# Asking for the background transfers on GpSimd's queue instead of the sync queue

## The chip, the core and the metric

The kernel runs on one core of a Trainium2 chip. A core has five engines that run side by side, each working through its own list of instructions in order: TensorE (PE, matrix products; its weight loads are PEld), VectorE (DVE), ScalarE (ACT), GpSimd (POOL) and SyncE (SP), which here does nothing but ask for transfers. An instruction waits at the head of its engine's list until the semaphores it needs are set, and everything behind it on that engine waits with it. That is true of a transfer's request as well: it stands in the list of the engine that issues it. The metric is device time of one execution in microseconds (us), lower is better.

## The reference: what is computed

One layer of a diffusion backbone over 2048 latent tokens of width 1024, with a context of 256 tokens ahead of them, all in float32:

```python
ada = silu(c) @ w_ada + b_ada            # 6 vectors of 1024: sh1, sc1, g1, sh2, sc2, g2
h   = modulate(rmsnorm(x, norm_mix), sh1, sc1)
o   = token_mixers(h @ w_in, ...)        # gated recurrence (4 heads) and gMLP gating (4 heads)
x   = x + g1 * (o @ w_out)
h2  = modulate(rmsnorm(x, norm_ffn), sh2, sc2)
x   = x + g2 * conv_ffn(h2, w_up, conv_w, conv_b, w_down)
out = rmsnorm(x, norm_final)
```

Of `ada`, the first two vectors are needed at once; `g1`, `sh2`, `sc2`, `g2` only after the token mixers. The kernel folds the gates into weights: `w_out * g1` and `w_down * g2` are formed once, in the background of the token mixers, and parked in DRAM.

## The kernel before, in words

The products are done in three float32r passes (high times high, high times low, low times high), so each weight tile is split into a high part (`S.copy` to `whi`, L125, on ACT) and a low part (`wlo`, L126, on DVE or POOL).

The first 960 us or so are the token mixers. TensorE projects `h` with 128 columns of `w_in` at a time: a bank is eight steps of three matmuls (`pj`). For each new group of columns a raw tile of 512 KB is loaded (L207, on SP), split, and used. Between the steps of a bank two pumps may each put in a piece of other work. One pump carries the heads: the recurrence's score products (`sc`), transposes (`mi`), norms and gates. The other, `bg_q`, carries the background, one generator after another:

- `ada_block(e)`, e = 0 to 7: 512 columns of `w_ada` for `g1`, `sh2`, `sc2`, `g2`. Four raw tiles of 512 KB (L877) are multiplied into a row sum on DVE (L885); the bias row comes first (L871), and four of the eight blocks store their result into the small DRAM tensor `g_d` (L895).
- `w_down_ops`: 22 pieces of `w_down` (L939), each multiplied by `g2` (L941, DVE) and stored to `wd_d` (L942); `g2` is read back twice from `g_d` (L936).
- `w_out_ops`: 16 pieces of `w_out` (L915) with the matching `g1` (L916), multiplied (L925, DVE), split (ACT, then DVE) and stored to `wo_d` in two halves (L927, L928).

A generator's `yield 7.0` means that its next piece is put in once about 7 us of matmuls have been written behind it. The background's raw tiles and the raw tiles of `w_in` are the same three buffers (`raw_tile`, tag `raw`, bufs=3), taken in turn. So a load of `w_in` may have to wait until a background piece has been stored out of the buffer that it gets.

The order on each engine is made by a scheduler when the program is built. It plays the program through with costs of its own and writes each engine's instructions down in the order in which they came up; `pin` fixes the relative order of some. On the chip this order is fixed, whatever the real times are.

POOL's own work in this part is small: the two steps of each reciprocal root (L118 a multiply-add, L120 a power), wanted by the norms of the recurrence's output (`on`, L698) and of the gating (`nt`, L671 and L673); the gating's last product (L647); and the zeroing of the row sums (L870). After the token mixers the background is done, and the rest of the kernel has none of the changed lines in it.

Of the kernel before, what the change touches and what calls it, by code (L numbers as in the profile page):

```python
# [18 lines left out]
P = 128  # L19
# [31 lines left out]
def view(t, off, dims):  # L51

    return bass.AP(t.tensor, t.offset + off, [list(t.ap[0])] + [list(d) for d in dims])
# [24 lines left out]
def tile_trunk(ctx, tc, x, c, cx, c_ctx, w_ada, b_ada, norm_mix, norm_ffn, w_in, hg_norm, sgu_g, sgu_b,  # L78
               w_sp, b_sp, w_out, w_up, conv_w, conv_b, w_down, norm_final, masks, out):
    nc = tc.nc  # L80
    V, S, G, T = nc.vector, nc.scalar, nc.gpsimd, Tensor(nc.tensor)
    ld = nc.sync.dma_start
    st = nc.sync.dma_start
    pin = tc.keep_in_program_order

    x = x[0]
    w_ada, w_in, w_out, w_up, w_down = w_ada[0], w_in[0], w_out[0], w_up[0], w_down[0]
# [19 lines left out]
    g_d = dr.tile([2, D], F32, name="g_d")  # L107
# [3 lines left out]
    wo_d = dr.tile([P, NK, 2, D], F32, name="wo_d")  # L111
    wd_d = [dr.tile([P, 2, D], F32, name=f"wd{j}") for j in range(NF // 2)]
# [10 lines left out]
    def split(hi, lo, raw, eng=None, keep=lambda i: i):  # L123

        keep(S.copy(hi, raw))  # L125
        (eng or G).tensor_sub(lo, raw, hi.bitcast(F32))  # L126
# [56 lines left out]
    with es1:  # L183
# [13 lines left out]
        def bank(tag):  # L197
            return ps.tile([P, 512], F32, tag=tag, name=tag, bufs={"pj": 3, "sc": 2, "mi": 3}[tag])

        def raw_tile():  # L200
            return p1.tile([P, D], F32, tag="raw", name="raw", bufs=3)
# [54 lines left out]
        acc = ph.tile([P, 2, 512], F32, tag="S", name="acc")  # L256
# [609 lines left out]
        def ada_block(e):  # L866

            col = 2 * D + e * 512
            acc = pm.tile([P, 512], F32, tag="acc", name="acc")
            G.memset(acc, 0.0)  # L870
            ld(acc[0:1, :], b_ada[0:1, col:col + 512])  # L871
            wts = []

            def load(k):
                if k < 8:
                    wt = raw_tile().rearrange("p (k c) -> p k c", k=2)
                    ld(wt, w_ada[:, col:col + 512].rearrange("(p k) e -> p k e", k=8)[:, k:k + 2, :])  # L877
                    wts.append(wt)
            load(0)
            yield 4.0  # L880
            for k in range(0, 8, 2):
                load(k + 2)
                wt = wts.pop(0)
                for i in range(2):
                    pin(V.scalar_tensor_tensor(out=acc, in0=wt[:, i, :], scalar=cs2[:, k + i, 0:1], in1=acc,  # L885
                                               op0=ALU.mult, op1=ALU.add))
                yield 3.2
            yield 3.0
            pa = bank("mi")
            hf_ = e % 2  # L890
            if e in (0, 1, 6, 7):
                T.matmul(pa[:1, :], ones[:, :1], acc, start=True, stop=True)
                gr = pm.tile([P, 512], F32, tag="ot", name="gr", bufs=2)
                S.copy(gr[:1, :], pa[:1, :])
                st(g_d[e // 6:e // 6 + 1, hf_ * 512:hf_ * 512 + 512], gr[:1, :])  # L895
            else:
                for j in range(4):
                    T.matmul(pa[:, 2 * j:2 * j + 2], acc[:, j * P:(j + 1) * P], ones[:, :2], start=True, stop=True)
                if e in (2, 3):
                    V.tensor_copy(s2[:, hf_ * 4:hf_ * 4 + 4], pa[:, 0:8:2])  # L900
                else:
                    V.scalar_tensor_tensor(out=a2[:, hf_ * 4:hf_ * 4 + 4], in0=pa[:, 0:8:2], scalar=1.0,
                                           in1=nffn[:, hf_ * 4:hf_ * 4 + 4], op0=ALU.add, op1=ALU.mult)
            yield 0.0

        def w_out_ops():

            todo = [(k, slice(n * 512, n * 512 + 512)) for k in range(NK) for n in range(2)]
            raws = []

            def load(i):
                if i < len(todo):
                    k, cl = todo[i]
                    raw = raw_tile()
                    ld(raw[:, :512], w_out[k * P:(k + 1) * P, cl])  # L915
                    ld(raw[:, 512:], g_d[0:1, cl].broadcast_to([P, 512]))  # L916
                    raws.append(raw)
            load(0)
            yield 5.0
            for i, (k, cl) in enumerate(todo):  # L920
                load(i + 1)
                raw = raws.pop(0)
                w, g = raw[:, :512], raw[:, 512:]
                hi = pm.tile([P, 512], F32, tag="acc", name="wo_hi")
                pin(V.tensor_mul(w, w, g))  # L925
                split(hi.bitcast(F32R), g.bitcast(F32R), w, V)
                st(wo_d[:, k, 0, cl], hi)  # L927
                st(wo_d[:, k, 1, cl], g)  # L928
                yield 7.0

        def w_down_ops():

            for n in range(2):
                cl = slice(n * 512, n * 512 + 512)
                g = pm.tile([P, 512], F32, tag="acc", name="g2")
                ld(g, g_d[1:2, cl].broadcast_to([P, 512]))  # L936
                for j in range(NF // 2):
                    raw = raw_tile().rearrange("p (a c) -> p a c", a=2)
                    ld(raw, w_down[2 * j * P:2 * (j + 1) * P, cl].rearrange("(a p) c -> p a c", p=P))  # L939
                    yield 9.0  # L940
                    pin(V.tensor_mul(raw, raw, view(g, 0, [[0, 2], [1, 512]])))  # L941
                    st(wd_d[j][:, :, cl], raw)  # L942
                    yield 2.5

        def silu(dst, scale):
# [6 lines left out]
        def head(hh, h):  # L952
# [16 lines left out]
            def pre_g():  # L969
                if prev[0] >= 0:  # L970
                    need(hg_q, (prev[0], prev[1], "keys"))
                else:
                    need(bg_q, "x1")
                    for e in range(8):
                        bg_q.add(ada_block(e))
                    bg_q.add(conv_taps())
                    bg_q.add(w_down_ops())
                    bg_q.add(w_out_ops())
                t["F"] = pk.tile([P, 2, TH], F32, tag="F", name="F", align_bytes=AL)
                t["K"] = pk.tile([P, 2, TH], F32, tag="K", name="K", bufs=2, align_bytes=AL)  # L980
# [125 lines left out]
    def ubank():  # L1106
        return ps2.tile([P, 512], F32, tag="up", name="up", bufs=4)
# [364 lines left out]
    for n, (u, i) in enumerate(prods):  # L1472
# [4 lines left out]
        p = ubank()  # L1477
        hi, lo = u.A[i]
# [19 lines left out]
        if n in (NP - 4, NP - 3, NP - 2):  # L1498
            j = n - NP + 4
# [198 lines left out]
    for n in range(3, 7 * NJ - NB):  # L1698
        q, j = divmod(n, NJ)
# [53 lines left out]
```

## Time and profile before

| what | value |
|---|---|
| three runs | 2442.68, 2446.64, 2447.78 us; median 2446.64 us |
| the profiled execution | 2442.51 us, of which the span of the trace is 2440.7 us |
| TensorE busy | 2373.1 us, 97% of the span |
| VectorE, ScalarE, GpSimd busy | 1713.6, 1030.0, 797.8 us |
| mean granted TensorE clock | 0.991 of full speed |
| transfers | 400.09 MB, 396.85 MB of it through one queue, that of SP |

The span runs from the first to the last instruction of the profiled execution. Busy time of an engine is the time in which one of its own instructions runs; requests for transfers are not counted as busy. In what follows a "wait" is idle time of an engine ahead of one instruction, put down to the instruction or transfer whose semaphore came last. A timeline lists instructions by start and length in us.

### The profile page before, as it was taken

What the parts mean: (1) busy time and instruction counts of PE and PEld (TensorE: products, weight loads), DVE (VectorE), ACT (ScalarE), POOL (GpSimd) and SP (SyncE); (2) the same over time, 40 slices, a digit from 0 to 9 for tenths busy, and PEclk for the clock granted to TensorE, in tenths of its full rate; (3) what the DMA queues carried; (4) which work ended last, traced back from release to release, by engine and by line L of the source; (5) the groups of instructions that cost most, each with busy time, mean ns of one, the idle gap of its engine ahead of it and who ended that gap; (6) DMA issues with size and microseconds to landing.
All of it is one profiled execution on the core that took longest, in us unless ns stands there. A gap on an engine that the chain in (4) does not pass through costs nothing.

```text
span 2440.7 us, 38853 instructions
## 1 busy us (share of the span) xinstructions
PE 2373.1 (97%) x14931; PEld 1939.1 (79%) x14931; DVE 1713.6 (70%) x2333; ACT 1030.0 (42%) x1780; POOL 797.8 (33%) x744
## 2 busy tenths in 40 slices
PE   7999999999999898999999999999999999999998
PEld 3787888878877777888788888878888887888887
DVE  5655774555676664566898777769999983676876
ACT  2774544544554543444433333333333342332343
POOL 1010000000000022002678878777787860000011
PEclk8999999999999999999999999999999999999999
DMA  8355444473436536668732222552222248843744
GB/s 292 106 182 168 151 141 137 156 251 128 145 113 216 172 127 229 193 209 265 259 93 85 87 91 85 203 209 85 94 85 94 84 157 326 296 140 130 250 151 173
DMA packets 306279, 400.09 MB, mean 164 GB/s; under 512 B 33697, under 2 KB 216729, under 8 KB 302381
## 3 DMA queue, kind: packets, MB, share of 16 engines
q1 hardware_dynamic: 302836, 396.85, 49.1%
q8 instruction: 118, 1.93, 0.3%
q10 hardware_dynamic: 3257, 0.75, 0.1%
q14 instruction: 68, 0.56, 0.1%
HBM read 288.41 MB, written 109.13 MB: 163 GB/s over the span
## 4 chain that ended last, share of the span: by engine, by line
PE 43%; DVE 7%; issue 1%; DMA 1%; ACT 1%; POOL 1%; SPq 0%; POOLq 0%; ACTq 0%; DVEq 0%
PE up L70 25%; PE dn L70 18%; DVE dn L1333 3%; DVE edges L1338 1%; DVE gp L1409 1%; ACT dn L1330 1%; DMA yfar<-yd 0%; DMA raw<-in_w_up_dram 0%; POOL Al L126 0%; DVE keep L1419 0%; DVE keep L1403 0%; ACT cv L1352 0%; ACT Ah L125 0%; DMA m<-cv 0%; PE up L74 0%
## 5 line engine op out<-in xcount | busy, mean ns | idle before, releaser
L1333 DVE SCALAR_TENSOR_TENSOR dn<-gp,taps,dn 128x1024 f32<-128x1024 f32 x352 | 448.2, 1280 | 21.0 <-ACT dn L1330 17.8
L70 PE MATMUL up<-yfar,Ah 128*128 128x512 f32 x1232 | 394.2, 390 | 2.9 <-DMA yfar<-yd 2.9
L70 PE MATMUL dn<-thl,mhl 128*128 128x512 f32 x1680 | 381.0, 389 | 0.0
L70 PE MATMUL pj<-xh,whi 128*128 128x512 f32 x896 | 368.3, 411 | 10.8 <-ACT whi L125 10.8
L126 POOL TENSOR_TENSOR Al<-raw,Ah 128x512 fp32r<-128x512 f32 x264 | 343.4, 1309 | 94.5 <-ACT Ah L125 89.1
L70 PEld LDWEIGHTS dn<-thl,mhl 128*128 128x128 f32 x1680 | 315.4, 188 | 65.5 <-issue 0.2
L70 PE MATMUL pj<-xh,wlo 128*128 128x512 f32 x896 | 354.0, 395 | 0.7 <-DVE wlo L126 0.7
L70 PE MATMUL pj<-xl,whi 128*128 128x512 f32 x896 | 354.6, 396 | 0.0
L125 ACT CAST Ah<-raw 128x512 fp32r<-128x512 f32 x264 | 160.5, 618 | 286.9 <-PE up L70 219.2
L70 PE MATMUL up<-xah,Al 128*128 128x512 f32 x704 | 275.9, 392 | 2.0 <-POOL Al L126 1.8
L70 PE MATMUL up<-xah,Ah 128*128 128x512 f32 x704 | 275.4, 391 | 1.8 <-ACT Ah L125 1.8
L70 PEld LDWEIGHTS up<-yfar,Ah 128*128 128x128 f32 x1232 | 231.2, 188 | 51.7 <-DMA yfar<-yd 3.7
L70 PEld LDWEIGHTS pj<-xh,whi 128*128 128x128 f32 x896 | 170.3, 190 | 48.1 <-ACT whi L125 11.7
L70 PE MATMUL up<-xal,Ah 128*128 128x512 f32 x528 | 206.3, 391 | 0.0
L70 PE MATMUL up<-yfar,Al 128*128 128x512 f32 x528 | 205.4, 389 | 0.0
L70 PEld LDWEIGHTS pj<-xh,wlo 128*128 128x128 f32 x896 | 169.8, 189 | 38.1 <-DVE wlo L126 1.6
L70 PEld LDWEIGHTS pj<-xl,whi 128*128 128x128 f32 x896 | 170.4, 190 | 30.6 <-DVE xl L126 0.5
L70 PE MATMUL dn<-wo,o 128*128 128x512 f32 x768 | 184.6, 397 | 3.2 <-DMA wo<-wo_d 2.2
L70 PEld LDWEIGHTS dn<-wo,o 128*128 128x128 f32 x768 | 143.2, 190 | 33.1 <-DMA wo<-wo_d 2.6
L126 DVE TENSOR_TENSOR wlo<-raw,whi 128x1024 fp32r<-128x1024 f32 x67 | 81.9, 1222 | 117.6 <-ACT whi L125 116.3
L70 PEld LDWEIGHTS up<-xah,Al 128*128 128x128 f32 x704 | 132.6, 188 | 33.0 <-POOL Al L126 5.7
L70 PEld LDWEIGHTS up<-xah,Ah 128*128 128x128 f32 x704 | 132.5, 188 | 29.9 <-ACT Ah L125 2.8
(320 smaller groups left out, 3698.6 us busy)
## 6 DMA issues: line engine op xcount, KB each, us to landing
raw<-in_w_up_dram SPq DMA_DIRECT2D x88, 512.0 KB
mr<-m SPq DMA_DIRECT2D x85, 512.0 KB
raw<-in_w_in_dram SPq DMA_DIRECT2D x68, 512.0 KB
sT<-wd SPq DMA_DIRECT2D x88, 256.0 KB
raw<-in_w_ada_dram SPq DMA_DIRECT2D x32, 512.0 KB
yfar<-yd SPq DMA_DIRECT2D x14, 1024.0 KB
m<-cv SPq DMA_DIRECT2D x22, 544.0 KB
raw<-in_w_down_dram SPq DMA_DIRECT2D x22, 512.0 KB
```

The lines of the kernel that those rows point to most:

```text
L70: return self.engine.matmul(out, lhsT, rhs, **kw)
L125: keep(S.copy(hi, raw))
L126: (eng or G).tensor_sub(lo, raw, hi.bitcast(F32))
L1330: S.activation(cr, gt[:, 0:RH, 0:GW], AF.Identity, bias=cvb[:, f:f + 1], scale=taps[:, f:f + 1])
L1333: V.scalar_tensor_tensor(out=cr, in0=gt[:, t // 3:t // 3 + RH, t % 3:t % 3 + GW], scalar=taps[:, t * NF + f:t * NF + f + 1], in1=cr, op0=A ...
L1338: V.scalar_tensor_tensor(out=e[:, 0, :], in0=gt[:, 1, t % 3:t % 3 + GW], scalar=taps[:, t * NF + f:t * NF + f + 1], in1=e[:, 0, :], op0=AL ...
L1409: V.tensor_add(g_rows(hh, f + c, n2), quad(p, kind), quad(add, kind))
```

## The change

A third name for requesting a transfer is added, `gd`, which issues on POOL. Every request of the three background generators, loads and stores alike, goes from `ld` or `st` (both SP) to `gd`. No tile, no size, no `yield` and no arithmetic is changed.

```diff
     ld = nc.sync.dma_start
     st = nc.sync.dma_start
+    gd = nc.gpsimd.dma_start
...
-            ld(acc[0:1, :], b_ada[0:1, col:col + 512])
+            gd(acc[0:1, :], b_ada[0:1, col:col + 512])
...
-                    ld(wt, w_ada[:, col:col + 512].rearrange("(p k) e -> p k e", k=8)[:, k:k + 2, :])
+                    gd(wt, w_ada[:, col:col + 512].rearrange("(p k) e -> p k e", k=8)[:, k:k + 2, :])
...
-                st(g_d[e // 6:e // 6 + 1, hf_ * 512:hf_ * 512 + 512], gr[:1, :])
+                gd(g_d[e // 6:e // 6 + 1, hf_ * 512:hf_ * 512 + 512], gr[:1, :])
...
-                    ld(raw[:, :512], w_out[k * P:(k + 1) * P, cl])
-                    ld(raw[:, 512:], g_d[0:1, cl].broadcast_to([P, 512]))
+                    gd(raw[:, :512], w_out[k * P:(k + 1) * P, cl])
+                    gd(raw[:, 512:], g_d[0:1, cl].broadcast_to([P, 512]))
...
-                st(wo_d[:, k, 0, cl], hi)
-                st(wo_d[:, k, 1, cl], g)
+                gd(wo_d[:, k, 0, cl], hi)
+                gd(wo_d[:, k, 1, cl], g)
...
-                ld(g, g_d[1:2, cl].broadcast_to([P, 512]))
+                gd(g, g_d[1:2, cl].broadcast_to([P, 512]))
...
-                    ld(raw, w_down[2 * j * P:2 * (j + 1) * P, cl].rearrange("(a p) c -> p a c", p=P))
+                    gd(raw, w_down[2 * j * P:2 * (j + 1) * P, cl].rearrange("(a p) c -> p a c", p=P))
...
-                    st(wd_d[j][:, :, cl], raw)
+                    gd(wd_d[j][:, :, cl], raw)
```

Counted from the loops, 154 requests move: 8 biases, 32 pieces of `w_ada`, 4 stores to `g_d`, 2 reads of `g2`, 22 loads and 22 stores of `w_down`, and 64 of `w_out` (16 pieces with two loads and two stores each). POOL's list grows from 669 rows to 823.

The first place is on POOL, in the `w_out` part, at the second pair of norms of a head that was put off (`rs<-oss`, the reciprocal root for `on`). Before, these were POOL's neighbours; in square brackets stand the semaphores that a row waits for, by the engine or transfer lane that sets them (DMAHW: a lane of SP's transfers):

```order
L118 TENSOR_SCALAR rs<-oss 128x4 [waits Activation_49,Pool_49]
L120 TENSOR_TENSOR rs_7540<-rs,mhalf 128x4 [waits DVE_49,Pool_49]
L118 TENSOR_SCALAR rs<-oss 128x4 [waits Activation_49,Pool_49]
L120 TENSOR_TENSOR rs_7737<-rs,mhalf 128x4 [waits DVE_49,Pool_49]
L118 TENSOR_SCALAR rs<-oss 128x4 [waits Activation_49,Pool_49]
L120 TENSOR_TENSOR rs_7773<-rs,mhalf 128x4 [waits DVE_49,Pool_49]
```

Now, with every line number one higher and DMASW for the lanes of POOL's transfers:

```order
L119 TENSOR_SCALAR rs<-oss 128x4 [waits Activation_49,Pool_49]
L121 TENSOR_TENSOR rs_7737<-rs,mhalf 128x4 [waits Pool_49]
L928 DMA wo_d<-wo_hi 128x512 [waits DMASW2_49,Activation_49]
L916 DMA raw<-in_w_out_dram 128x512 [waits DMAHW3_49,DMASW1_49,DVE_49]
L929 DMA wo_d<-raw 128x512 [waits DMASW4_49,DVE_49]
L119 TENSOR_SCALAR rs<-oss 128x4 [waits Activation_49,Pool_49]
L917 DMA raw<-g_d 128x512 [waits DMASW5_49]
L121 TENSOR_TENSOR rs_7773<-rs,mhalf 128x4 [waits Pool_49]
```

Two stores and two loads of the background now stand between the norms' steps, one load between the two steps of the same root.

The second place is on SP, around the first load of `w_in` after the middle of the `w_out` part (`Qb`, `bs` and `op` are the parked operands of a head that was put off, `oT` the mixers' output). Before:

```order
L927 DMA wo_d<-wo_hi 128x512 [waits DMAHW4_49,Activation_49]
L928 DMA wo_d<-raw 128x512 [waits DVE_49]
L915 DMA raw<-in_w_out_dram 128x512 [waits DMAHW6_49,DMAHW1_49]
L916 DMA raw<-g_d 128x512 [waits DMAHW7_49]
L927 DMA wo_d<-wo_hi 128x512 [waits DMAHW0_49,Activation_49]
L928 DMA wo_d<-raw 128x512 [waits DVE_49]
L207 DMA raw<-in_w_in_dram 128x8x128 [waits DMAHW5_49,DMAHW2_49]
L845 DMA Qb<-qb_354 128x1024 [waits DMAHW3_49]
```

Now the same load of `w_in` (L208, the first of the two rows) has only work of the heads ahead of it:

```order
L847 DMA op<-op_358 128x1024 [waits PE_49,Activation_49]
L845 DMA bs_8628<-dh_362 128x1024 [waits DVE_49,DMAHW1_49,PE_49,Activation_49]
L846 DMA Qb<-qb_354 128x1024 [waits DMAHW2_49]
L848 DMA Qb<-sg_366 128x1024
L208 DMA raw<-in_w_in_dram 128x8x128 [waits DMAHW4_49,DMAHW7_49,DMASW5_49,DVE_49]
L208 DMA raw<-in_w_in_dram 128x8x128 [waits DMAHW5_49,DMAHW7_49,DMASW7_49,DVE_49]
```

The six rows of `w_out` are gone from SP, the reads of `Qb` have moved ahead of the weights, and the weights wait for a lane of POOL's transfers beside the others.

## Rows read from the trace of the kernel before

**Rows 1.** Page: busy time by engine, and the chain that ended last.
```profile
PE 2373.1 (97%) x14931; PEld 1939.1 (79%) x14931; DVE 1713.6 (70%) x2333; ACT 1030.0 (42%) x1780; POOL 797.8 (33%) x744
...
PE 43%; DVE 7%; issue 1%; DMA 1%; ACT 1%; POOL 1%; SPq 0%; POOLq 0%; ACTq 0%; DVEq 0%
```

**Rows 2.** Windows: stretch, length, busy us by engine, clock, DMA share, GB/s.
```profile
706.00:890.00 184.00, 170.39 (x1642) 140.61 (x1641) 117.38 (x208) 91.76 (x204) 23.84 (x28) 0.96 0.52 168
...
sum 784.00, PE 758.25 PEld 621.58 DVE 489.72 ACT 377.56 POOL 67.53; mean PE 189.56 PEld 155.40 DVE 122.43 ACT 94.39 POOL 16.88
...
772.00:778.00 6.00, 6.00 (x84) 4.77 (x84) 4.53 (x6) 1.15 (x2) 0.00 (x0) 0.72 0.87 256
```

**Rows 3.** Waits of PE, 176 to 960 us: total, times, longest.
```profile
PE pj L70 <- ACT whi L125: 7.8, 2, 6.2
PE mi L74 <- DVE on L698: 3.7, 4, 1.3
...
PE mi L74 <- ACT vv L561: 1.9, 1, 1.9
```

**Rows 4.** Waits of SP's queue, 176 to 960 us: total, times, longest.
```profile
SPq L942 <- DVE raw L941: 91.8, 19, 15.2
...
SPq L207 <- DMA wd<-raw: 23.5, 10, 4.8
...
SPq L207 <- DMA wo_d<-raw: 9.4, 5, 3.4
```

**Rows 5.** Timeline of SP's queue, 798 to 846 us: start, length, instruction.
```profile
829.61 0.32 SPq L928 DMA_DIRECT2D wo_d<-raw  x1
...
832.21 0.43 SPq L207 DMA_DIRECT2D raw<-in_w_in_dram  x1
```

**Rows 6.** Timeline of ACT, 838 to 843 us; in brackets, idle before and releaser.
```profile
838.55 1.04 ACT L125 CAST whi<-raw 128x1024 fp32r<-128x1024 f32 x1 [3.92 <-DMA raw<-in_w_in_dram]
```

**Rows 7.** Timeline of PE, 836 to 856 us.
```profile
839.65 0.80 PE L70 MATMUL pj<-xh,whi 128*128 128x512 f32 x1 [6.19 <-ACT whi L125]
...
843.23 0.63 PE L70 MATMUL pj<-xl,whi 128*128 128x512 f32 x1
```

**Rows 8.** Timeline of PE, 768 to 784 us.
```profile
771.97 0.66 PE L74 MATMUL mi<-ident,vv 128*128 128x128 f32 x4 [1.93 <-ACT vv L561]
772.46 0.60 PE L74 MATMUL mi<-ident,on 128*128 128x128 f32 x4
...
773.26 0.63 PE L70 MATMUL pj<-xl,whi 128*128 128x512 f32 x1
773.69 0.63 PE L70 MATMUL pj<-xh,wlo 128*128 128x512 f32 x1
...
776.54 0.39 PE L70 MATMUL pj<-xh,whi 128*128 128x512 f32 x1
```

**Rows 9.** Timeline of POOL, 760 to 773 us.
```profile
767.03 0.19 POOL L118 TENSOR_SCALAR rs<-oss 128x4 f32<-128x4 f32 x1 [3.49 <-ACT ojk L695]
767.31 1.01 POOL L120 TENSOR_TENSOR rs<-rs,mhalf 128x4 f32<-128x4 f32 x1
```

**Rows 10.** Timeline of SP's queue, 760 to 774 us.
```profile
766.70 0.32 SPq L928 DMA_DIRECT2D wo_d<-raw  x1
770.20 0.33 SPq L915 DMA_DIRECT2D raw<-in_w_out_dram  x1
```

**Rows 11.** Timeline of DVE, 766 to 773 us.
```profile
768.35 0.69 DVE L698 TENSOR_TENSOR on<-op,rs 128x512 f32<-128x512 f32 x1 [1.68 <-POOL rs L120]
```

**Rows 12.** Groups of POOL: count, busy us, mean ns, idle before.
```profile
L120 POOL TENSOR_TENSOR rs<-rs,mhalf 128x4 f32<-128x4 f32 (+1 forms) x47 | 44.0, 935 | 5.5 <-DVE on L698 1.8 <-ACT nt L673 0.2
...
L647 POOL TENSOR_TENSOR nt<-nt,gu 128x512 f32<-128x512 f32 x16 | 26.7, 1667 | 92.6 <-ACT gu L652 71.0 <-DVE nt L681 9.4 <-DVE mv L667 8.4
```

**Rows 13.** Timelines of POOL and DVE, 884 to 894 us.
```profile
887.65 4.35 POOL L647 TENSOR_TENSOR nt<-nt,gu 128x512 f32<-128x512 f32 x1 [6.96 <-ACT gu L652]
...
886.98 2.21 DVE L477 TENSOR_TENSOR Q<-Q,F 128x1024 f32<-128x1024 f32 x1
```

## The prediction, made before the changed kernel was run

> **What bounds the kernel now.** I read the page first: TensorE is busy for 97% of the span, and in the chain that ended last the queues (SPq, POOLq, ACTq) stand at 0% [rows 1]. So a transfer's request is worth something only where TensorE waits for what it brings. The changed lines run between about 176 us and 890 us, so I asked next for windows up to 960 us, when the last head is done. The four windows sum to 784.00 us with TensorE busy for 758.25 us, which leaves 25.75 us, 1.1% of the kernel. That is the ceiling of everything that better timing of transfers can remove here. POOL is busy for 67.53 us of the same 784 us [rows 2]. So there is room on POOL, and hardly any gain on TensorE.
>
> The waits of TensorE in that stretch show who holds it [rows 3]. The largest group is the projection waiting for weights (`whi`): 7.8 us in two waits, the longer 6.2 us. Then come the transposes waiting for the norm's output `on` (3.7 us in four) and a transpose waiting for `vv` (1.9 us). SP's queue, read last, waits far more: 91.8 us for `w_down` pieces that DVE has yet to multiply; and 23.5 us in ten and 9.4 us in five of its waits are loads of `w_in` held up by a background store that must land before the shared raw buffer is free [rows 4]. The reader is to see that SP's queue is full of waits of which TensorE notices almost none.
>
> One more thing prices a wait. After the 1.93 us wait at 771.97 us, matmuls start 0.43 us apart (773.26 to 773.69) and run 0.63 us each; at 776.54 they are back at 0.39 us [rows 8]. The window from 772 to 778 us has a granted clock of 0.72 with TensorE busy throughout, so part of it ran at the lower level (1.2 GHz) and 0.28 x 6 = 1.7 us were lost [rows 2]. The long wait at 839.65 us is followed by the same: 0.63 us a matmul at 843.23 us [rows 7]. A wait of about 2 us therefore costs nearly 4. I take 1.7 us per new wait of 2 us or more, and the same back for one that goes.
>
> **The change, part by part.** 154 requests leave SP and come to POOL. No byte and no arithmetic changes, so three things can: what SP's queue does sooner, what POOL's own work does later, and when a background transfer lands.
>
> *SP's side, a gain.* A request takes 0.32 to 0.43 us on SP [rows 5], so about 154 x 0.37 = 57 us of issue leave it, at no value by themselves, since SP isn't on the chain. The value is where weights were late. The long wait was TensorE at 839.65 us for `whi`, which ACT could cast only at 838.55 us after 3.92 us of waiting for the load of `w_in` [rows 6], which SP had asked for at 832.21 us, behind stores of `w_out` that were held until 829.61 us and later [rows 5]. Freed of them, SP could ask up to 832.21 - 829.61 = 2.6 us sooner. Not more, I think: the load's buffer is one that a background piece must leave first, which is why the new order shows it waiting on a lane of POOL's transfers. Bounds: 0, if the buffer is the limit anyway, and 6.2 + 1.7 = 7.9 us, if the wait goes altogether with its slow clock. I take 2.5 us, near the 2.6 us that the rows show.
>
> *POOL's side, a loss.* The trace has no transfer requested by POOL. From below, a request costs what it costs SP, 0.32 us [rows 5]. From above I use POOL's longest instruction here, a product of 512 columns that took 4.35 us, against a mean of 1.67 us for its sixteen [rows 12, 13]. I take 1.0 us, near POOL's power on four columns (0.94 us, nearly all of it fixed) [rows 12]. Then 154 x 1.0 = 154 us come to 67.53 busy us in 784: they fit. In the densest part, 706 to 890 us, 64 requests of `w_out` join 23.84 busy us in 184 [rows 2]: they fit too.
>
> What costs is not the sum but the order. At the place shown in the change, the root for `on` (767.03 us, then the power at 767.31 us [rows 9]) now stands behind a store that was ready at 766.70 us and, worse, behind a load of `w_out` that could be asked for only at 770.20 us [rows 10]; and the power stands behind the next load. At 1.0 us a request: load 770.20 to 771.20, the store to 772.20, root to 772.39, the other load to 773.39, power to 774.40, `on` (0.69 us [rows 11]) to 775.1. Before, `on` ended at 769.04 us, and TensorE wanted it at 772.46 us [rows 8]. TensorE's order is the same here, so it waits some 2.6 us more. It is at the lower clock there already, so I add little for that: 3 us. Bounds: 0, if the buffer comes free sooner, and 2.6 + 4 x (1.67 - 1.0) + 1.7 = 7 us at the longer mean. Elsewhere POOL has nothing for some us ahead of a root (its norms wait for ACT, as the 3.49 us at 767.03 us [rows 9]), and that idle time hides requests that are ready; if it were gone, each would cost its 1.0 us in the norm's path.
>
> *Landing.* Fifteen loads of `w_in` already wait for a background store [rows 4]. A store from POOL starts later by the difference in issue, 1.0 - 0.32 = 0.7 us, and perhaps later by more. Only two waits for weights reached TensorE [rows 3], so I charge 2 x 0.7 = 1.4 us, rounded to 1. Bounds: 0, and all fifteen at 0.7 us, 10 us.
>
> The sum is -2.5 + 3 + 1 = +1.5 us on the profiled execution's 2442.51 us, so 2444. That execution lies 4.1 us under the median of the three runs, 2446.64 us, so for a median I say 2448 us. No change can be told from one under 0.2%, here 4.9 us either way, so this counts as the same.
>
> **A rule against it.** POOL and DVE are in each other's way at one place: POOL's product took 4.35 us while DVE ran a product of two operands in SBUF for 2.21 us from 886.98 us [rows 13]. The Trainium skill ("SBUF — State Buffer", section "SBUF: two separate sides") says that a transfer requested on GpSimd has its descriptors written by GpSimd's cores, which a DVE instruction in a two-port mode locks out, and advises the ACT or SP queue. It also says that a product of two tensors has no such mode and collides only with a GpSimd instruction that reads SBUF; with this the 4.35 us agree. No run here shows yet whether a request is held up; by the warning the 1.0 us would be several times as much, by the exception it would stand.
>
> **The rivals.**
>
> *POOL's queue overflows (slower).* Each request is stretched by DVE as the product was. The point from which this decides: 64 requests of `w_out` plus 23.84 us of its own fill the 184 us from 706 to 890 us at (184 - 23.84) / 64 = 2.5 us each [rows 2]. From there every root in that stretch is late by more than the one before. For it: POOL's 4.35 us beside DVE [rows 13], and DVE busy for 117 of the 184 us. Against it: the mean of the sixteen products is 1.67 us [rows 12], and a request need not read SBUF. Price: five places where TensorE wants a norm, each 2 us late with 1.7 us of slow clock, about +19 us: 2466 us.
>
> *Weights come later (slower).* The shared buffers pass on the delay of the stores. For it: 32.9 us of loads of `w_in` waiting for stores now [rows 4], and the new order, in which they wait for POOL's lanes. Against it: only two of the waits for weights reach TensorE. It decides when a store lands over 1.5 us later than now; if four more of the fifteen then come through, 4 x (1.5 + 1.7) = +13 us: 2460 us.
>
> *The weights come sooner (faster).* SP, without waits for DVE at its head, asks for `w_in` and `Qb` as early as the buffers allow; the wait of 6.2 us goes with its slow clock, -7.9 us, and the delay at 767 us does not come about because the buffer is free earlier: about 2438.5 us. For it: the 91.8 us in which SP's head stood waiting for DVE [rows 4]. Against it: the buffers are the same three.
>
> That nothing moves at all, because each request waits for the same data on either queue, falls under the forecast.
>
> **How the numbers follow.** The forecast, no change, gets 0.40; POOL's overflow 0.20; late weights 0.15; weights sooner 0.25. Faster is then 0.25, the same 0.40, slower 0.35. The forecast's own range is 2443 to 2452 us. The range to 8 in 10 takes in most of the faster case, late weights, and the overflow near its point of decision: 2437 to 2464 us.
>
> **What would show it.** POOL's requests should each hold its queue for about 1 us; 2.5 us or more speaks for the overflow. The wait for `whi` near 840 us should be shorter, by about 2.5 us. TensorE should wait for `on` near 772 us. SP's waits for `w_down` and `w_out` should be gone from its list and stand on POOL. The loads of `w_in` that wait for a store should be about as many as before. The forecast is wrong if TensorE's idle time between 176 and 960 us moves by more than 5 us from 25.75, or if the rest of the kernel, which has none of the changed lines, changes its length.

## The result, and the profile after

The changed kernel takes 2453.48 us (median of 13 runs, 2449.70 to 2456.56), the kernel before 2446.21 us (13 runs, 2442.68 to 2450.62). The ratio is 1.0029, with a 95% interval of 1.0021 to 1.0038: slower by 0.29%, some 7 us. A second set of five runs gave 1.0044 (1.0031 to 1.0057). The predicted 2448 us was 5.5 us low. The wide range, 2437 to 2464 us, held the time; the forecast's own, 2443 to 2452 us, did not. The profiled execution after took 2452.87 us with a span of 2451.1 us, near its median, while that of before lay 4 us under its own; so the two traces differ by 10.4 us, about 3 us more than the medians do.

The page after, busy time, chain and queues, which answers to [rows 1]:

```profile
PE 2374.4 (97%) x14931; PEld 1939.6 (79%) x14931; DVE 1718.5 (70%) x2333; ACT 1028.5 (42%) x1780; POOL 897.6 (37%) x898
...
q1 hardware_dynamic: 272636, 339.67, 41.3%
q0 software_dynamic: 16608, 57.18, 7.1%
...
PE 40%; DVE 7%; issue 1%; POOL 1%; DMA 1%; ACT 1%; SPq 0%; POOLq 0%; ACTq 0%; DVEq 0%
```

57.18 MB went through POOL's own queue. POOL is busy for 99.8 us more: here its requests do count as busy, 154 of them, 0.64 us on average.

Windows of the w_out part and the sum of the same four stretches as in [rows 2]:

```profile
706.00:890.00 184.00, 170.15 (x1635) 139.71 (x1634) 115.83 (x210) 88.43 (x201) 58.92 (x93) 0.95 0.50 163
...
sum 784.00, PE 756.26 PEld 618.50 DVE 490.16 ACT 372.91 POOL 163.89; mean PE 189.07 PEld 154.63 DVE 122.54 ACT 93.23 POOL 40.97
```

TensorE idles 27.74 us of the 784, only 2 more than before. That is not all that it lost: a matmul at the lower clock counts as busy, and the same 784 us hold a little less of the work. Its waits in that stretch have changed their names, against [rows 3]:

```profile
PE mi L74 <- ACT vv L562: 5.7, 2, 3.1
PE mi L74 <- DVE on L699: 4.4, 5, 1.4
...
PE pj L70 <- DMA xl<-xl_d: 2.1, 3, 0.8
PE mi L70 <- ACT K L534: 2.0, 1, 2.0
...
PE pj L70 <- ACT whi L126: 1.2, 1, 1.2
```

The 6.2 us wait for weights is gone, and `vv`, 1.9 us before, now costs 5.7 us. On SP's queue the waits for DVE of [rows 4] have left, and those for buffers have grown from 23.5 and 9.4 us:

```profile
SPq L208 <- DMA wd<-raw: 129.4, 11, 38.3
...
SPq L208 <- DMA wo_d<-raw: 73.5, 9, 13.7
```

On POOL's queue, the same stretch, stand the waits that SP had:

```profile
POOL wd L943 <- DVE raw L942: 102.0, 20, 15.8
...
POOL wo_d L928 <- ACT wo_hi L126: 50.1, 9, 14.8
```

SP comes to its loads sooner and waits there for the same buffers. That is what freeing a queue looks like when buffers are the limit.

**Where it is lost: two places.** The first is the end of the program. After the last store SP must meet the other engines. The waits of SP's queue from 2436 us on, before and then after:

```profile
SPq L1749 <- PEq L1749: 0.6, 2, 0.4
```

```profile
SPq L1750 <- PEq L1750: 3.9, 2, 3.4
```

The profile gives this wait to TensorE's queue, which had long been done. The engine that came last is POOL: its last instruction, a drain that the program's end puts on every engine, takes 8.03 us after against 0.66 us before (the trace has these lengths; no view prints them). SP is through at 2447.09 us, POOL only at 2450.29 us, and the next step of the end follows at 2450.33 us. The wait is 3.3 us longer (3.9 against 0.6), for nothing that the kernel computes, and it is a part of the span in which nothing was changed.

The second is the w_out part. ACT there after, its weights' casts and `vv` copies:

```profile
772.67 1.05 ACT L126 CAST whi<-raw 128x1024 fp32r<-128x1024 f32 x1 [6.01 <-DMA raw<-in_w_in_dram]
...
777.52 0.58 ACT L562 COPY vv<-pj 128x512 f32<-128x512 f32 x1
...
788.71 1.04 ACT L126 CAST whi<-raw 128x1024 fp32r<-128x1024 f32 x1 [9.28 <-DMA raw<-in_w_in_dram]
789.66 0.58 ACT L562 COPY vv<-pj 128x512 f32<-128x512 f32 x1
```

And the same casts and copies on ACT before:

```profile
767.65 1.05 ACT L125 CAST whi<-raw 128x1024 fp32r<-128x1024 f32 x1 [0.77 <-DMA raw<-in_w_in_dram]
...
771.33 0.58 ACT L561 COPY vv<-pj 128x512 f32<-128x512 f32 x1
...
777.43 0.59 ACT L561 COPY vv<-pj 128x512 f32<-128x512 f32 x1 [4.19 <-PE pj L70]
...
781.64 1.05 ACT L125 CAST whi<-raw 128x1024 fp32r<-128x1024 f32 x1 [2.62 <-DMA raw<-in_w_in_dram]
```

Before, both `vv` copies ran ahead of the second cast. After, the scheduler wrote that cast between them; on the chip its load was not there yet, ACT stood still for 9.28 us, and the second copy, which waited for nothing else, came 12.2 us later than before, of which 5.6 us are the distance of the two profiles at 762 us. TensorE after, which answers to [rows 7, 8]:

```profile
778.15 0.66 PE L74 MATMUL mi<-ident,vv 128*128 128x128 f32 x4 [2.52 <-ACT vv L562]
...
790.29 1.12 PE L74 MATMUL mi<-ident,vv 128*128 128x128 f32 x4 [3.14 <-ACT vv L562]
...
850.73 0.79 PE L70 MATMUL pj<-xh,whi 128*128 128x512 f32 x1 [1.19 <-ACT whi L126]
```

### The profile page after: what moved, and what is told of

The parts are those of the page before. It is cut to its first block, busy times and chain, and to the rows that moved or that the text cites. A ratio compares the mean times of both kernels' runs of the same rounds, so it can differ in the third digit from the quotient of the medians.

```text
span 2451.1 us, 38956 instructions
## 1 busy us (share of the span) xinstructions
PE 2374.4 (97%) x14931; PEld 1939.6 (79%) x14931; DVE 1718.5 (70%) x2333; ACT 1028.5 (42%) x1780; POOL 897.6 (37%) x898
## 3 DMA queue, kind: packets, MB, share of 16 engines
q0 software_dynamic: 16608, 57.18, 7.1%
## 4 chain that ended last, share of the span: by engine, by line
PE 40%; DVE 7%; issue 1%; POOL 1%; DMA 1%; ACT 1%; SPq 0%; POOLq 0%; ACTq 0%; DVEq 0%
PE up L70 23%; PE dn L70 17%; DVE dn L1334 4%; DVE edges L1339 1%; DVE gp L1410 1%; POOL Al L127 1%; ACT dn L1331 0%; DMA yfar<-yd 0%; POOL raw L1160 0%; DVE keep L1420 0%; DVE keep L1404 0%; DMA xn<-cv 0%; ACT cv L1353 0%; POOL cv L1421 0%; POOL fl L1156 0%
## 5 line engine op out<-in xcount | busy, mean ns | idle before, releaser
L70 PE MATMUL up<-yfar,Ah 128*128 128x512 f32 x1232 | 394.2, 390 | 4.1 <-DMA yfar<-yd 3.8
L70 PE MATMUL dn<-thl,mhl 128*128 128x512 f32 x1680 | 381.0, 389 | 0.0
L70 PE MATMUL pj<-xh,whi 128*128 128x512 f32 x896 | 368.1, 411 | 4.9 <-ACT whi L126 4.2
L70 PEld LDWEIGHTS dn<-thl,mhl 128*128 128x128 f32 x1680 | 315.2, 188 | 65.6 <-issue 0.2
L70 PE MATMUL pj<-xl,whi 128*128 128x512 f32 x896 | 354.7, 396 | 2.2 <-DMA xl<-xl_d 2.1
L70 PE MATMUL pj<-xh,wlo 128*128 128x512 f32 x896 | 353.5, 395 | 0.0
L70 PE MATMUL up<-xah,Al 128*128 128x512 f32 x704 | 275.1, 391 | 3.0 <-POOL Al L127 2.9
L70 PE MATMUL up<-xah,Ah 128*128 128x512 f32 x704 | 274.6, 390 | 1.8 <-ACT Ah L126 1.8
L70 PEld LDWEIGHTS up<-yfar,Ah 128*128 128x128 f32 x1232 | 231.1, 188 | 53.5 <-DMA yfar<-yd 4.8
L70 PE MATMUL up<-xal,Ah 128*128 128x512 f32 x528 | 205.4, 389 | 0.0
L70 PE MATMUL up<-yfar,Al 128*128 128x512 f32 x528 | 205.3, 389 | 0.0
L70 PEld LDWEIGHTS pj<-xh,whi 128*128 128x128 f32 x896 | 170.3, 190 | 42.7 <-ACT whi L126 4.7
L70 PEld LDWEIGHTS pj<-xh,wlo 128*128 128x128 f32 x896 | 169.8, 190 | 37.1 <-DVE wlo L127 0.8
L70 PEld LDWEIGHTS pj<-xl,whi 128*128 128x128 f32 x896 | 170.4, 190 | 33.7 <-DMA xl<-xl_d 3.4
L70 PE MATMUL dn<-wo,o 128*128 128x512 f32 x768 | 184.6, 397 | 2.9 <-DMA wo<-wo_d 2.0
L70 PEld LDWEIGHTS dn<-wo,o 128*128 128x128 f32 x768 | 143.1, 189 | 32.9 <-DMA wo<-wo_d 2.4
L70 PEld LDWEIGHTS up<-xah,Al 128*128 128x128 f32 x704 | 132.2, 188 | 34.5 <-POOL Al L127 7.2
L70 PEld LDWEIGHTS up<-xah,Ah 128*128 128x128 f32 x704 | 132.2, 188 | 29.7 <-ACT Ah L126 2.8
```

The costliest lines, as they stand in the source:

```text
L70: return self.engine.matmul(out, lhsT, rhs, **kw)
```

## Experiments

All were timed in 5 rounds, each beside the kernel before on the same chip. The theories have letters: A, a fixed price at the end once POOL has asked for a transfer; B, the w_out part alone; C, a price for each request; later D, a drain that grows with the number of requests, and E, ACT's order.

**One request, and each generator alone.** Four kernels: before with a single bias on POOL, then only w_ada, only w_down, only w_out.

```diff
-            ld(acc[0:1, :], b_ada[0:1, col:col + 512])
+            (gd if e == 0 else ld)(acc[0:1, :], b_ada[0:1, col:col + 512])
```

The other three keep the changed lines of one generator and take `ld` and `st` back in the others.

> The kernel before with one request of the 154 on POOL (the bias of the first block of w_ada); every engine's order is that of before. Theory A (a fixed price at the end of the program once POOL has asked for a transfer, here or after the last store): the last store lands as before and the span ends some 6.6 us behind its request instead of 2.8, so +3.5 us, about 2449.7 us against 2446.2. Theory B (all of the loss lies in the w_out part, 762 to 791 us, where buffers are passed on later) and theory C (a price for every request, 7.1 us / 154 = 0.05 us each): no change, 2446.2 us, and an end like that of before.

Measured: 2448.26 against 2447.89 us, ratio 1.0001 (0.9991 to 1.0011). The last drain takes 0.74 us. A falls: one request costs nothing.

> Only the 44 requests of w_ada (pieces, biases, stores to g_d) on POOL. A: +3.5 us (2449.7), all of it behind the last store; B: 0 (2446.2); C: 44 x 0.05 = +2 us, spread over 176 to 490 us. TensorE's matmuls between 176 and 487 us should keep the pace of before (within 1 us) for A and B.

Measured: ratio 1.0002 (0.9993 to 1.0012). The drain takes 4.27 us, but SP is still busy with its last stores until then, so nothing of it shows.

> Only the 46 requests of w_down on POOL. A: +3.5 us (2449.7) at the end and nothing else; B: 0; C: +2.1 us. If the new waits for xl near 487 to 526 us (+1.8 us in the changed kernel) belong to w_down's stores, A comes to +5.3 us (2451.5) with them.

Measured: ratio 1.0002 (0.9992 to 1.0011); drain 4.44 us, of which 0.25 us stands out behind SP.

> Only the 64 requests of w_out on POOL. A with B: the end costs 3.5 us, the stretch from 762 to 791 us +6.9 (weights of w_in asked for 5 to 8 us later, vv late behind their cast on ACT), the stretch from 791 to 858 us gives 4 back, so about +6.4 us (2452.6). B alone: +2.9 us (2449.1). A alone: +3.5 us with TensorE's pace from 706 to 890 us that of before. C: +3.0 us.

Measured: ratio 1.0008 (0.9998 to 1.0018), under what A with B expected; B alone or C alone would fit it. The drain takes 5.90 us and SP waits at the end:

```profile
SPq L1750 <- PEq L1750: 1.9, 2, 1.7
```

The waits of TensorE from 735 to 800 us show the second place again, with none of the other 90 requests on POOL:

```profile
PE mi L74 <- ACT vv L562: 5.0, 2, 3.0
```

**Is the drain counted in requests?** With w_ada and w_down on POOL, w_out not (90 requests):

> w_ada and w_down on POOL (90 requests), w_out on the sync queue. So far POOL's last drain took 0.66, 0.74, 4.27, 4.44, 5.90 and 8.03 us for 0, 1, 44, 46, 64 and 154 requests: 0.082 us each up to 64, and for 154 as much as 90 would cost. Theory D (the drain pays for requests not yet cleaned up): 8.03 us if it saturates at 90 (span ends 3.2 us after the sync queue is through, about +3.5 us in all), 2.8 us and hidden if requests are cleaned up in lots of 64 (26 left, about +0.5 us). Theory B (w_out's order costs 6.9 us between 762 and 791 us): that stretch is as before here, within 1.5 us. If instead all requests have a price in the token mixers, TensorE is 3 to 4 us behind at 960 us.

Measured: ratio 1.0009 (0.9999 to 1.0020); the drain takes 2.80 us, the figure of the second form. From 742 to 791 us it is like before (table below), so that loss needs w_out on POOL. TensorE's wait for weights near 840 us is there again, in its waits from 791 to 905 us:

```profile
PE pj L70 <- ACT whi L126: 6.3, 1, 6.3
```

Then 154 requests that carry nothing:

```diff
             ld(nf, norm_final.rearrange("(o d) -> o d", o=1).broadcast_to([P, D]))
+            for i in range(154):
+                G.dma_start(g_d[0:1, 4 * i:4 * i + 4], nf[0:1, 4 * i:4 * i + 4])
```

> The kernel before with all its transfers on the sync queue, and 154 requests of 16 bytes more on POOL, in the down stage where POOL has nothing else from 2040 to 2280 us (they write a row of g_d that nobody reads any more). The other engines' order is that of before. Theory D by number of requests: the last drain takes 8.0 us (or 13.3 if it doesn't saturate), and the span ends 3.2 (8.5) us later than before for no other reason; median +3.2 us (+8.5). If the drain goes by packets or bytes: under 1.5 us and no change of the time. Theory B alone: no change.

Measured: ratio 0.9995 (0.9985 to 1.0004); the drain takes 3.38 us, hidden. Neither number was expected: 8.0 by count, under 1.5 by size. So a request leaves something behind whatever it carries, but these small ones left less. Among the large ones it goes by count and not by size: w_ada's 44 requests and w_out's 64 moved some 16.8 MB each, and left 4.27 and 5.90 us. The lengths of POOL's last drain, by number of requests (the last line is 0.66 us and 0.082 us for each request left; 0.082 is (4.27 - 0.66) / 44):

```
requests   0     1     44    46    64    90    122   154
us         0.66  0.74  4.27  4.44  5.90  2.80  5.41  8.03
left       0     1     44    46    64    26    58    90
computed   0.66  0.74  4.27  4.43  5.91  2.79  5.42  8.04
```

The last three fit if one lot of 64 had been cleaned up by then. Why two lots were not at 154, and what the small requests do, stays open.

**Can it be paid earlier?**

```diff
+        if n == 8:
+            pin(G.drain())
         if n == 2 * NJ - 3:
             ld(nf, norm_final.rearrange("(o d) -> o d", o=1).broadcast_to([P, D]))
```

The loop is that of the down stage; `pin` puts the drain behind all of POOL's work written so far.

> The changed kernel with one more drain of POOL in the down stage, where POOL has nothing to do; every other order is that of the changed kernel. Theory D: the early drain takes about 8 us and holds nobody, the last one takes 0.7 us, and the span ends 3.2 us sooner after the last store: about 2450.3 against the changed kernel's 2453.5 (ratio to before 1.0016 instead of 1.0029). If the length of the last drain is a fixed price of POOL's queue having been used, the last drain stays at 8 us and the time at 2453.5.

Measured: 2450.92 us, ratio 1.0016 (1.0005 to 1.0027). The early drain takes 8.74 us at 2022 us. POOL's product before it still runs for the first 1.3 us of that, as the last instruction does for 0.6 us of the 8.03 us, so the drain itself is 7.4 us long at either time. From 2041 us to the end TensorE keeps its pace within 0.1 us of before. In the 33 us around the drain it loses 1.7 us on the first profile of before, and 0.2 us in the kernel with both remedies below; kernels without an early drain lie between -0.2 and 2.2 us there. The last one takes 0.66 us, and SP's wait at the end is that of before:

```profile
SPq L1752 <- PEq L1752: 0.6, 2, 0.5
```

D stands: the price is moved to where it costs nothing that can be told from scatter. The ratio falls from 1.0029 to 1.0016, about 3.2 us. The two intervals overlap a little, so this rests on the trace, where SP's wait at the end is 3.3 us shorter, more than on the medians.

**What is late near 780 us?** The w_out stores go back to SP, the loads stay on POOL:

```diff
-                gd(wo_d[:, k, 0, cl], hi)
-                gd(wo_d[:, k, 1, cl], g)
+                st(wo_d[:, k, 0, cl], hi)
+                st(wo_d[:, k, 1, cl], g)
```

> The changed kernel, but the two stores of each w_out piece go back to the sync queue; its loads stay on POOL (122 requests there). Theory B in this form: a store that is ready stands behind loads that wait for a buffer at POOL's head, the buffer it empties is late for the next load of w_in, ACT waits for that load ahead of vv. With the stores off POOL the loads of w_in are asked for 4 us or more sooner near 764 and 776 us and TensorE's loss from 762 to 791 us falls from 6.9 to under 3 us. If the loss comes from how late a transfer by POOL lands, or from the two engines' queues meeting anywhere, it stays at 5 to 7 us. Drain: 122 - 64 = 58 or saturated at 90: 5.4 or 8.0 us.

Measured: ratio 1.0008 (0.9998 to 1.0018), drain 5.41 us. The loss stays at 6.5 us, TensorE's waits from 735 to 800 us:

```profile
PE mi L74 <- ACT vv L562: 7.5, 2, 5.8
```

A store behind a load on POOL is not the cause. What all kernels run so far with w_out's loads on POOL share here, and no other has, is the order on ACT, the cast ahead of the second `vv`. So that order alone was undone:

```diff
-            split(hi, lo, raw, eng or V)
+            n_split.append(key); split(hi, lo, raw, eng or V, pin if len(n_split) == 60 else lambda i: i)
```

On ACT this moves one cast behind the second `vv`, the copy `near` and one `wo_hi`; on DVE and POOL one neighbouring pair each swaps with it.

> The changed kernel with one cast moved on ACT: the cast of the weights that came between the two vv copies in the w_out part now stands behind both, as in the kernel before. TensorE's and SP's orders are the same. Theory E (the loss from 762 to 791 us is ACT's order: with w_out's loads on POOL the weights' cast was written ahead of vv, and ACT waits 9 us at it for a load that is not there yet): TensorE's wait of 3.1 us for vv near 790 us goes, with its slow clock, and the stretch from 742 to 791 us loses 2 to 4 us less than the 5 to 7 seen with w_out on POOL. Of the kernel's time 0 to 3 us, since the later stretch gave most of that back anyway: 2450 to 2453. If the loss is the late load itself (the buffers), TensorE waits as long, for whi instead of vv.

Measured: 2453.24 us, ratio 1.0028 (1.0019 to 1.0037). The second wait for `vv` is gone, TensorE's rows:

```profile
779.75 1.12 PE L74 MATMUL mi<-ident,vv 128*128 128x128 f32 x4 [3.07 <-ACT vv L562]
...
788.16 0.60 PE L74 MATMUL mi<-ident,vv 128*128 128x128 f32 x4
```

and on ACT its copy runs when its data is there, ahead of the cast:

```profile
785.38 0.59 ACT L562 COPY vv<-pj 128x512 f32<-128x512 f32 x1 [3.89 <-PE pj L70]
...
790.71 1.05 ACT L126 CAST whi<-raw 128x1024 fp32r<-128x1024 f32 x1 [3.74 <-DMA raw<-in_w_in_dram]
```

E is right about the place and worth nothing in the total that can be told from noise: as the table shows, it loses 5.3 us less than the changed kernel up to 791 us, but wins back only 1.3 us by 905 us where that one wins back 5.5.

**Both remedies, another queue, and the changed kernel again.**

> Both remedies in the changed kernel: the cast behind vv, and POOL's drain in the down stage. If both mechanisms are the loss: last drain 0.7 us, 3.2 us from that and 0 to 3 us from the cast, 2447 to 2450, a ratio to before of 1.000 to 1.0015; under 1 it would beat both kernels. If a price for each request is left: 1.0015 to 1.002.

Measured: 2448.83 us, ratio 1.0009 (1.0000 to 1.0019). Better than the changed kernel, not better than before. Its interval overlaps that of the early drain alone (1.0016), so what the cast adds is not settled.

```diff
-    gd = nc.gpsimd.dma_start
+    gd = nc.scalar.dma_start
```

> All 154 requests on ACT's queue instead of POOL's. No drain to pay on POOL (0.7 us, as before). If only POOL's kind of queue costs, this is the kernel before within 2 us, or faster if freeing SP is worth something (2443 to 2448). If a request's price is what stands behind it on its engine, it is slower: the background's stores wait for DVE for 90 us at the queue's head, and behind them stand the casts that TensorE waits for; with 10 of 40 such waits reaching TensorE at 2 us each, +20 us: 2467.

Measured: 2449.11 us, ratio 1.0009 (0.9998 to 1.0021): no price of 20 us, and no gain. The last drain is 0.66 us. SP has none of the 154 requests, as in the changed kernel, yet the wait near 840 us is there in full, from TensorE's waits, 791 to 905 us:

```profile
PE pj L70 <- ACT whi L126: 6.0, 1, 6.0
```

> The changed kernel once more, for the scatter of its stages: the last drain 8.0 us again and the span's end 3.2 us after the sync queue is through; waits of 2 to 4 us for vv near 780 and 790 us again; 2453 us, ratio 1.003. The first 42 us, which hold no changed line, were 2.5 us longer in its first profile than before's; if that is scatter, they lie anywhere from 0 to 2.5 us here.

Measured: 2457.32 us (5 runs), ratio 1.0044 (1.0031 to 1.0057); drain 8.02 us, SP's wait at the end 3.9 us again, `vv` 7.3 us in two. The first 42 us, which hold no changed line, were 2.1 us longer than in the first profile of before; over all profiles that stretch scatters from 0 to 2.5 us.

**Where each profile loses.** For every stretch, how much later TensorE's n-th matmul starts than in the first profile of before, end less beginning (us; the stretches are named by times in that profile):

```
                           212-487  487-526  526-742  742-791  791-905  sum
before's order   before       0        0        0        0        0       0
                 one bias     0.0      0.1     -0.2     -1.2      0.9    -0.5
                 dummies     -0.3      1.2     -0.2     -1.3      0.7     0.0
w_out alone on POOL          -0.3      3.0      0.2      6.7     -3.9     5.6
w_ada and w_down on POOL      0.4      1.3      0.2      1.2     -0.7     2.3
w_out stores on SP            0.4      2.3      1.4      6.5     -7.8     2.9
all on POOL      first        0.3      1.8      0.9      6.9     -5.5     4.3
                 again        0.7      2.8      1.2      6.1     -4.3     6.5
                 early drain  0.3      0.9      2.6      4.8     -4.7     3.9
                 vv first     0.7      1.9      1.0      1.6     -1.3     3.8
                 both         0.9      1.7      0.8      1.7     -3.2     1.8
```

Five profiles with all requests on POOL lose 4.1 us on average in the token mixers, three of before's order -0.2. With 3.3 us at the end that is the 7 us. The largest entry, 742 to 791 us, is mostly paid back by 905 us. Of the rest no single stretch stands clear of the scatter: w_out alone, which has before's order and queues up to 706 us, shows 3.0 us from 487 to 526 us. Three profiles are not in the table: w_ada alone lost 1.6 us in the token mixers, w_down alone 2.7, all requests on ACT -0.3. These are single profiles, and in two longer stretches without a changed line, 960 to 1200 and 1200 to 2041 us, the same comparison gives -4.0 to 2.7 and 1.0 to 4.4 us. So the 4.1 us are as large as such scatter; what speaks for them is that all five profiles lose, and that the medians are 7.3 us apart of which the end explains 3.3. Theory C, a price for each request, is not excluded for this part: 7.1 us / 154 would be a ratio of 1.0008 for w_ada, 1.0009 for w_down, 1.0012 for w_out and 1.0017 for the 90, and every one of these lies inside the measured interval.

## Why the prediction was right and where it was not

The time came out inside the range, on the far side of the 0.2% that the forecast allowed. That is in part luck: the range was wide for the sake of rivals that did not come as described, and nearly half of the loss lies where the prediction had nothing. Point by point:

- *The sum of three terms, +1.5 us.* Mis-sized: the token mixers lost 4.1 us on average over five profiles (1.8 to 6.5). The missing part has no one place, and its cause stays open. The sign set for it, idle time that moves by more than 5 us, stayed silent at 2.0 us.
- *The rest of the kernel at nothing.* This step failed. The prediction named it as a sign of being wrong, and it was: 3.3 us lie at the program's end, where the drain of POOL pays for requests made 1500 us earlier. The early drain shows it.
- *SP's side, -2.5 us.* The wait near 840 us did go, 6.2 to 1.2 us, more than priced, with 2.0 us for `K` appearing beside it. But the reason given was wrong. It went in every kernel with w_out's loads on POOL (1.0 to 2.2 us left), even where SP kept w_out's stores, and stayed at 6.0 us when all requests went to ACT, which frees SP as much. The weights came no sooner: the order that the scheduler wrote for TensorE fills the gap. Before, TensorE is through with the transposes of `on` at 833.46 us and begins its bank 6.19 us later, at 839.65 us [rows 7], with sixteen products `mi<-bs,Qb` behind that:

  ```profile
  832.86 0.60 PE L74 MATMUL mi<-ident,on 128*128 128x128 f32 x4
  ...
  841.53 1.05 PE L70 MATMUL mi<-bs,Qb 128*128 128x128 f32 x4
  ...
  854.16 0.60 PE L70 MATMUL mi<-bs,Qb 128*128 128x128 f32 x4
  ...
  855.98 1.05 PE L70 MATMUL mi<-bs,Qb 128*128 128x128 f32 x8
  ```

  After, it is through at 844.43 us and begins the same bank 6.30 us later, at 850.73 us, but the sixteen products stand in between, 3.08 us of work:

  ```profile
  843.83 0.60 PE L74 MATMUL mi<-ident,on 128*128 128x128 f32 x4
  846.46 3.08 PE L70 MATMUL mi<-bs,Qb 128*128 128x128 f32 x16 [2.03 <-ACT K L534]
  ```

  All seven profiles with w_out's loads on POOL have this order and none of the other seven has it. SP asked for that load 1.25 us before TensorE was through with `on` before (832.21 us [rows 5]) and 1.1 us after it now, so not sooner but 2.4 us later:

  ```profile
  845.54 0.38 SPq L208 DMA_DIRECT2D raw<-in_w_in_dram  x1
  ```

  No run moved these products alone. That the buffers are the limit was foreseen as a bound, and SP's longer waits for stores show it: twenty of its loads wait for a store, 202.9 us in all, against fifteen and 32.9 us.
- *POOL's side, +3 us at 767 us.* The place was right and the engine wrong. POOL, which answers to [rows 9, 10]:

```profile
774.53 0.62 POOL L928 DMA_DIRECT2D wo_d<-wo_hi  x1 [6.91 <-ACT wo_hi L126]
775.27 0.54 POOL L916 DMA_DIRECT2D raw<-in_w_out_dram  x1
775.87 0.54 POOL L929 DMA_DIRECT2D wo_d<-raw  x1
776.48 0.34 POOL L119 TENSOR_SCALAR rs<-oss 128x4 f32<-128x4 f32 x1
776.89 0.59 POOL L917 DMA_DIRECT2D raw<-g_d  x1
777.50 1.04 POOL L121 TENSOR_TENSOR rs<-rs,mhalf 128x4 f32<-128x4 f32 x1
```

  The root does stand behind the store and the load, and the power behind another load. Yet the root's own input was ready only at 775.9 us, since ACT was held by the cast. With 0.2 us from input to root, as in the kernel with the stores on SP, and 0.28 us from root to power [rows 9], the power would have started at 776.4 us: POOL's queue cost it 1.1 us. TensorE waited 0.61 us for `on`, not 2.6 more.
- *A request's price, 1.0 us.* It was 0.64 us on average: 0.54 us for w_out, 0.72 us for the loads of w_ada and w_down, 0.97 us at most in any run. That is nearer to the lower bound, 0.32 us. Nor is POOL's power "nearly all" fixed: on one column, at the end of the kernel before, it takes 0.55 us.
- *Landing, +1 us.* The page after prints a time to land only for POOL's transfers (4.5 us for a piece of w_ada), so the difference to SP's could not be read. Late weights did reach TensorE, but through ACT's order and as `vv`: a wait for `whi` was the wrong name to count.
- *The rivals.* The overflow didn't come: no request took over 0.97 us, although DVE ran beside them as much as before. The Trainium skill's warning ("SBUF — State Buffer", section "SBUF: two separate sides") that DVE's two-port modes hold up such requests was hardly put to the test here: of DVE's 796 instructions between 176 and 960 us, 646 take two tensors and only six are copies or operations with a scalar. One request, the first bias, ran beside such an operation:

  ```profile
  200.03 0.92 POOL L872 DMA_DIRECT2D acc<-in_b_ada_dram  x1
  ...
  200.10 1.42 DVE L232 TENSOR_SCALAR xk<-xk,rs 128x1024 f32<-128x1024 f32 x2 [5.39 <-POOL rs L121]
  ```

  It took 0.92 us, the other seven biases 0.51 to 0.60 us, and it ended 0.10 us after the first of the two operations did. All eight profiles with w_ada on POOL show this (0.92 to 0.93 us). That agrees with the warning, at one place and for 0.4 us. It isn't shown to be the cause: with one bias alone on POOL the request came behind both operations and still took 0.75 us. The exception for products of two tensors (section "Who interferes with whom") agrees with the trace: 63 requests ran beside nothing else on DVE and took 0.62 us on average, 28 ran beside an idle DVE and took 0.63 us. Late weights did come, at 790 us, by way of ACT's order. Early weights did not: what was won at 840 us is TensorE's own order. The two nearly cancelled.

## What to carry to other kernels

A request moved to another queue also moves what a scheduler believes about the transfer, and with it the written order of engines that the change doesn't touch: compare the order of every engine before and after, for a wait placed ahead of data that is ready, and for work that moved into a wait. Requests on POOL's queue are paid once more at the program's end, where the profile blames another engine; look at the last 10 us, and if POOL works until the end, put a drain in a stretch where it idles. Where buffers set the pace, freeing the queue that waits for them only makes it wait longer.

## What the runs showed of the hardware that was not expected

- POOL's last drain takes 0.66 us without requests and 0.082 us more for each one left over: 4.27 us for 44, 5.90 us for 64, 8.03 us for 154. It does not shrink with time: with w_ada alone the last request was made at 408 us, with w_out alone at 890 us, the drain began some 2440 us into the kernel, and either paid 0.082 us for each. A drain in between empties it.
- It falls in lots: 90 requests left 2.80 us, less than 46 did (4.44 us). 154 requests of 16 bytes left 3.38 us, which none of the counts explains. That a lot is 64 is worked out from these lengths alone.
- What a request costs POOL hardly goes with its size: 0.72 us for a load of 512 KB, 0.54 us for 256 KB, 0.52 us for 16 bytes.
- ACT bore 154 requests without a measurable loss (1.0009, 0.9998 to 1.0021), though stores that wait for DVE stood ahead of its other work: 12.4 us of ACT's idle time between 176 and 960 us ended with a product of w_down on DVE.
